# A hybrid attention block on one Trainium2 core: other order of the first chunks, gates computed earlier, low parts ahead of sums, one GpSimd product on VectorE

## The chip, the cores and the metric

The kernel runs on one core of a Trainium2 chip. The core's engines work side by side, each through its own queue in order: TensorE (PE: matmuls, and the loading of their weights, PEld), VectorE (DVE), ScalarE (ACT), GpSimd (POOL) and SyncE (SP), which here issues nearly all DMA transfers. The metric is the time of one execution on the device, in microseconds; less is better. Before the change it is 2038.04 us, the median of three runs (2036.83 to 2039.37).

## The reference

One residual layer over 512 tokens of width 2048, in float32. Heads are 128 wide, eight of each kind.

```python
h = rmsnorm(x, g_attn)
proj = h @ w_in                        # qa, ka, va, qf, kf, vf, f_logit
log_f = log_sigmoid(f_logit + b_f)
o_sb  = stick_breaking_attention(qa, ka, va)
o_fox = forgetting_attention(qf, kf, vf, log_f)   # scores + c_t - c_s, c = cumsum(log_f)
x = x + concat(headnorm(o_sb), headnorm(o_fox)) @ w_out
u = relu(rmsnorm(x, g_mlp) @ w_up)
y = rmsnorm(x + (u * u) @ w_down, g_final)
```

## The kernel before, in words

**Precision.** Each float32 operand is split into a high part, rounded to the matmul's format (`fp32r`), and a low part, the rest. ScalarE makes the high part by a cast, VectorE the low part by a subtraction (`Piece.cast` L166, `Piece.low` L170, `split` L56). A product is three matmuls (`mm3`, L75 to L78): high by high, high by low, low by high. High and low parts of weights lie in three rotating slots (tags `wh`, `wl`, `hi_lo` L67), the raw weights, as they come from memory, in three slots of the tag `wraw` (`Piece.load`, L159). Whoever takes a slot waits until its last user is done.

**Order.** A `Plan` (L143) holds pairs of a planned time and a function, and runs them sorted by time. Inside a `manual_schedule` the named engines keep the order so written. From L184 to L601 that holds for TensorE, ScalarE, VectorE and SyncE; from L602 to L1040 for the first three only, and there the scheduler places SyncE's transfers itself. The planned times only order the work: each engine starts an instruction as soon as its operands are there.

**Value phase** (L209 to L599). Sixteen chunks of 128 columns of x are turned by TensorE (`turn_x`, four transposes into one PSUM bank), scaled and split into `hH` and `hL` (`x_high` L253 on ScalarE, `x_low` L256 on VectorE), with some further copies for the later products (`x_more`, `x_right`, `x_sum`). Each chunk is multiplied at once with its 264 columns of W_in, the values of the first two heads and the eight gate logits (`first_part` L290, `first_values` L296): twelve matmuls a chunk. The order of chunks is 0, 8, 1, 9, 2, 10, and so on (`seq`, L301); chunks 0, 8, 1, 9 have a raw weight tile each, later ones a tile for the pair k, k + 8, all in `wraw` slots. `begin` (L310) is SyncE's list of first loads, of x and weights by turns. `keep_busy` (L286) puts matmuls without use on TensorE. Then the values of the other heads follow in two groups of seven products each, with sums of quadrants in place of the eighth (L415 to L599). In the second group, which begins at the planned time TV + END, each product takes four pieces of weights: a cast on ScalarE, a low part and for four of the seven products sums on VectorE. SyncE stores the results to `vd` (`added`, L520). Two pieces of the first head's query and one of its key are loaded and split here too (`first_pieces`, L208).

**Attention phase** (L602 to L1040). Its period is TPER = 27.05 us for each of 16 heads (order: forget heads 6, 7, 0 to 5, then the stick-breaking ones). In period n TensorE projects query and key of head n from four pieces of W_in (`q_piece`, `project` L199; pieces of head n have n and a = 0 to 3 in the loop from L961), computes scores of head n - 1 and the product with values of head n - 2. In the first period the plan also has the gates (L647 to L679): from the gate logits the log-forget sums, `cq` by rows, and `ckd` in memory, from which each forget head reads `cb`. Beside it W_out is loaded, summed and split for later (`WeightSums` L873, `whole` L911 for the first four row groups, `half` L924); these sums and low parts are VectorE's, and `whole` keeps its quadrants in `mixed`, over the place of value-phase tiles.

**Tail** (L1800 to L1895). The last row block: four products of 512 columns, the last in two halves; for each, VectorE adds the residual, ScalarE squares, and GpSimd multiplies by `g_final` (L1824), but for the last, which VectorE multiplies in halves (L1826). Then comes the row's norm and the store.

Of the kernel before, what the change touches and what calls it, by code (L numbers as in the profile page):

```python
# [8 lines left out]
F32 = mybir.dt.float32  # L9
# [27 lines left out]
def block_kernel(ctx, tc, x, g_attn, w_in, b_f, g_out_sb, g_out_fox, w_out, g_mlp, w_up, w_down, g_final, y):  # L37
# [167 lines left out]

    first_pieces = [q_piece(0, which, half) for which, half in ((0, 0), (0, 1), (1, 0))]
    with ExitStack() as stage:
# [96 lines left out]
        pieces = {}  # L304
        for j in (0, K8, 1, K8 + 1):
            pieces[j] = Piece(w_rows[j % K8][:, j // K8:j // K8 + 1, c0:c0 + m], 1, m), 0
# [8 lines left out]
        for k in range(K8):  # L315
            t, j = mm_at[k], k + K8
            for jj, dt in ((k, 0.0), (j, step)):
                if k == 0:
                    for part, wait in zip(("hh", "hl", "lh"), (0.0, 0.6, 1.1)):
                        plan.at(t + dt + wait, first_part, jj, *pieces[jj], part)  # L320
                    continue
# [3 lines left out]
            if k == 0:  # L325
                w8 = pieces[8][0]
                jobs = [(-64.5, keep_busy, 9), (-5.0, turn_x, k), (-4.9, keep_busy, 3), (-4.1, w.cast), (-4.0, x_high, k),
                        (-3.9, w.low), (-3.5, x_low, k), (-3.3, x_more, k), (0.1, turn_x, j), (0.2, w8.cast), (0.25, x_high, j),
                        (0.3, w8.low), (0.4, x_low, j), (0.6, x_sum, j), (0.85, x_right, j)]
            elif k == 1:  # L330
                w9 = pieces[9][0]
                jobs = [(-1.9, turn_x, k), (-1.85, w.cast), (-1.8, x_high, k), (-1.6, w.low), (-1.5, x_low, k), (-0.75, x_more, k),
                        (-0.8, turn_x, j), (-0.4, w9.cast), (-0.3, x_high, j), (0.3, w9.low), (0.4, x_right, j), (0.85, x_low, j), (1.6, x_sum, j)]
            else:
                dt = mm_at[k - 1] - t
                jobs = [(-2.95, turn_x, k), (-2.2, x_high, k), (-1.5, x_low, k), (-0.75, x_more, k),
                        (-1.02, turn_x, j), (-0.3, x_high, j), (0.4, x_right, j), (0.85, x_low, j), (1.6, x_sum, j),
                        (dt - 1.5, w.cast), (dt - 0.05, w.low)]
                if k > 3:
                    jobs.append((-14.0, w.load))  # L340
            for dt, f, *args in jobs:
                plan.at(t + dt, f, *args)
# [183 lines left out]
        r1s = [None]  # L526

# [74 lines left out]
    manual = tc.manual_schedule(engines={pe.engine, act.engine, dve.engine})  # L602
    manual.__enter__()
# [10 lines left out]
    with tc.tile_pool(name="att", bufs=1, side="right", reuse_waits="tile") as at, \  # L614
# [6 lines left out]
        utri = at.tile([P, P], F32R, name="utri")  # L621
        onesr = at.tile([P, P], F32R, name="onesr")
        rb = at.tile([P, NT], F32, name="rb")
        cq = at.tile([P, TB, NH], F32, name="cq")
        lf = at.tile([P, TB, 2 * NH], F32R, name="lf")
        fe = at.tile([P, TB, NH], F32, name="fe")
        r1, fl = r1s[0], gates
# [3 lines left out]
        tri = at.tile([P, P], F32, tag="uh5", name="tri")  # L631
        pool.memset(tri, 0.0)
        pool.affine_select(out=tri, in_=tri, compare_op=ALU.is_gt, fill=1.0, base=0, pattern=[[-1, P]], channel_multiplier=1)
        one = at.tile([P, P], F32, tag="ul5", name="one")
        pool.memset(one, 1.0)
# [10 lines left out]

        def gates_1():  # L647
            for t in range(TB):
                dve.scalar_tensor_tensor(fl[:, t, :], fl[:, t, :], r1[:, t:t + 1], bf, op0=ALU.mult, op1=ALU.add)
            dve.tensor_copy(utri, tri)  # L650
            dve.tensor_copy(onesr, one)

        def gates_2():
            act.activation(fe, fl, AF.Abs)
            act.activation(fe, fe, AF.Exp, scale=-1.0)
            act.activation(fe, fe, AF.Ln, bias=1.0)
            dve.scalar_tensor_tensor(fl, fl, 0.0, fe, op0=ALU.min, op1=ALU.subtract)
            split(lf[:, :, :NH], lf[:, :, NH:], fl)

        def gates_3():  # L660
            cps = now["cps"] = atp.tile([P, TB, 2 * NH], F32, tag="o", name="cps")
            for t in range(TB):
                for i in range(t + 1):
                    pe.matmul(cps[:, t, :], utri if i == t else onesr, lf[:, i, :], start=(t == 0 and i == 0),
                              stop=(i == t), skip_group_check=True)

        def gates_4():
            act.copy(cq, now["cps"][:, :, :NH])
            dve.tensor_tensor(cq, cq, now["cps"][:, :, NH:], op=ALU.add)

        def gates_5():
            cT = now["cT"] = atp.tile([P, NT], F32, tag="o", name="cT")
            for t in range(TB):
                pe.transpose(cT[:NH, t * P:(t + 1) * P], cq[:, t, :], ident)

        def gates_6():
            ckT = at.tile([NH, NT], F32, tag="ul4", name="ckT")
            act.mul(ckT, now["cT"][:NH, :], -1.0)
            sp.dma_start(ckd, ckT)  # L679
# [50 lines left out]
        class Head:  # L730
# [41 lines left out]
            def plan_fox(self, plan, t):  # L772
# [28 lines left out]
                for dt, f in ((-4.0 if self.i else -1.5, load), (10.85, start), (14.6, maxed), (16.8, soft), (20.1, scale)):  # L801
                    plan.at(t + dt, f)
# [108 lines left out]
        def whole(m, t):  # L911
            w = WeightSums(m, (0, 1), lambda: mixed[:, :NH].rearrange("p (q a) n -> p q (a n)", a=2))
            loads, first, second = ((-15.0, 2.7), (21.5, 22.3, TPER + 3.3), (TPER + 1.75, TPER + 2.5, TPER + 6.7)) if m else \
# [6 lines left out]
            for dt, f in ((second[2] + 0.1, lambda: w.store(0, 2)), (TPER + 9.2, lambda: w.sum(2)), (TPER + 17.5, lambda: w.sum(3)),  # L920
                          (2 * TPER + 1.75, w.high_6), (2 * TPER + 2.5, w.low_6), (2 * TPER + 2.6, lambda: w.store(2, 4))):
                plan.at(t + dt, f)

        def half(m, d, n):  # L924
# [3 lines left out]
            jobs = [(17.6 if n == 8 else 8.3, w.load)]  # L928
            if d == 0:
                c, a = (23.2, (1.75, 2.4, 3.1, 3.8, 5.6, 6.4)) if n > 7 else (16.4, (5.5, 6.3, 7.0, 9.0, 12.0, 17.4))  # L930
                jobs += [(c, lambda: w.high(0)), (c + 0.7, lambda: w.low(0)), (c + 1.2, lambda: w.sum(0)), (c + 2.0, lambda: w.sum(1))]
# [29 lines left out]
        for n in range(2 * NH + 1):  # L961
            t = TPER * n
            i_s, i_o = n - 1, n - 2
            if n < 2 * NH:
                pieces = []
                for a, (which, hf) in enumerate(((0, 0), (0, 1), (1, 0), (1, 1))):
# [4 lines left out]
                    if n == 1 and a == 0:  # L971
                        cast, low = -7.0, -5.0
                    if n == 0:
                        cast, low = 16.3, 18.2
                    pieces.append(q_piece(n, which, hf).plan(plan, t + cast - 16, t + cast, t + low))
# [25 lines left out]
            if 0 <= i_s < 2 * NH:  # L1001
# [29 lines left out]
        for dt, f in ((16.25, widen_r1), (17.0, turn_r1), (17.5, lambda: act.copy(rb, now["rb"])), (17.1, gates_1), (17.9, gates_2), (21.5, gates_3),  # L1031
                      (22.0, gates_4), (24.2, gates_5), (24.8, gates_6)):
# [7 lines left out]
    manual.__exit__(None, None, None)  # L1040

    up_cm.__exit__(None, None, None)
    for cm in acc_cms[::-1]:
        cm.__exit__(None, None, None)
# [763 lines left out]
    def last_product(t, n, *banks):  # L1808
# [9 lines left out]
        for j, (ps, cols) in enumerate(zip(banks, parts)):  # L1818
# [4 lines left out]
            if len(parts) == 1:  # L1823
                pool.tensor_tensor(x2_, x2_, gf[:, n * NT:(n + 1) * NT], op=ALU.mult)  # L1824
            else:
                scaled = dve.tensor_tensor(last_piece[:, cols], x2_, gf[:, n * NT:(n + 1) * NT][:, cols], op=ALU.mult)  # L1826
# [10 lines left out]
    def last_row(t):  # L1837
# [20 lines left out]
        else:  # L1858
            m = [x2(t, 0), x2(t, 1), x2(t, 2), last_piece]
# [19 lines left out]
    last_piece = spare.tile([P, NT], F32, name="last")  # L1879
# [60 lines left out]
```

## Time and profile before

| | |
|---|---|
| median of three runs | 2038.04 us |
| lowest, highest | 2036.83, 2039.37 us |
| the profiled execution | 2037.16 us |
| its span, first to last instruction | 2035.1 us |
| TensorE busy | 2017.4 us, 99% of the span |
| VectorE busy | 1739.8 us, 85% |
| ScalarE busy | 1128.1 us, 55% |
| GpSimd busy | 64.5 us, 3% |
| mean granted TensorE clock | 0.998 |

All stretches and moments below are of the profiled execution, in us from the first instruction. A row of the timeline has the start, the duration, the engine, the line, the operation, the output, its inputs and the count; in brackets stands the idle time of the engine just before it and what ended it. "PE accq L78 <- DVE wl L171: 2.5, 1, 2.5" in the list of waits is: TensorE at L78 waited for VectorE's L171, 2.5 us in total, once, 2.5 at the longest. In the windows view each engine's busy time is followed by its count of instructions, and the last three columns are the granted clock, the busy share of the DMA engines and GB/s.

### The profile page before, as it was taken

The page shows a single profiled execution, that of the slowest core. Times are in us where ns is not written, and L with a number is a line of the kernel's source. Part 1 is how long each engine was busy: PE and PEld are TensorE (multiplying, and loading weights), DVE is VectorE, ACT ScalarE, POOL GpSimd, SP SyncE. Part 2 cuts the span into 40 slices and gives each one's busy share as a digit, 9 for nine tenths or more (in the row PEclk, how much of TensorE's full clock was granted, in tenths as well). Part 3 has the DMA queues.
Part 4 walks back from the last instruction along what each step waited for, and adds up shares of the span by engine and source line. Part 5 has one row for each costly group of instructions (what it writes and reads, how often), then busy time and mean ns, then how long its engine had stood idle before and what let it go on. Part 6 is the DMA issues. An engine that isn't in the chain of part 4 may idle for free.

```text
span 2035.1 us, 27208 instructions
## 1 busy us (share of the span) xinstructions
PE 2017.4 (99%) x10422; PEld 1744.6 (86%) x10422; DVE 1739.8 (85%) x1969; ACT 1128.1 (55%) x1619; POOL 64.5 (3%) x73
## 2 busy tenths in 40 slices
PE   8999999999999999999999999999999999999998
PEld 8998888888888889888888888888888888888887
DVE  7876777888867588899999999998799888888896
ACT  6543454455555566667667677676644344444444
POOL 0000001100000000000000000000000000000004
PEclk9999999999999999999999999999999999999999
DMA  6426666666538981766666666667685674674642
GB/s 225 164 98 221 198 203 189 211 202 197 183 119 278 301 268 65 234 182 187 211 207 189 215 193 211 198 197 257 241 299 197 225 260 169 235 253 176 222 162 85
DMA packets 270210, 413.45 MB, mean 203 GB/s; under 512 B 10312, under 2 KB 166008, under 8 KB 263552
## 3 DMA queue, kind: packets, MB, share of 16 engines
q1 hardware_dynamic: 269328, 409.61, 60.7%
q8 instruction: 82, 1.34, 0.3%
q10 hardware_dynamic: 752, 2.11, 0.3%
q14 instruction: 48, 0.39, 0.1%
HBM read 315.19 MB, written 96.49 MB: 202 GB/s over the span
## 4 chain that ended last, share of the span: by engine, by line
PE 93%; DVE 3%; DMA 1%; ACT 1%; issue 1%; POOL 0%; SPq 0%; ACTq 0%; POOLq 0%; DVEq 0%
PE psa L1175 10%; PE accd L77 8%; PE accd L78 8%; PE accd L76 8%; PE accq L76 5%; PE accq L78 5%; PE accq L77 5%; PE psa L1173 5%; PE psc L1175 5%; PE psc L1173 3%; PE psb L1175 3%; PE m L77 1%; PE m L76 1%; PE m L78 1%; PE psb L1173 1%; PE vy L78 1%
## 5 line engine op out<-in xcount | busy, mean ns | idle before, releaser
L1752 ACT CAST wh<-wd 128x1024 fp32r<-128x1024 f32 x126 | 124.9, 999 | 169.3 <-PE accd L78 54.6
L1642 DVE TENSOR_TENSOR wl<-wu,wh 128x1024 fp32r<-128x1024 f32 x158 | 192.6, 1220 | 13.0 <-ACT wh L1636 13.0
L78 PE MATMUL accq<-hH,wl 128*128 128x512 f32 x512 | 200.6, 392 | 2.5 <-DVE wl L171 2.5
L76 PE MATMUL accq<-hH,wh 128*128 128x512 f32 x512 | 202.2, 395 | 0.0
L77 PE MATMUL accq<-hL,wh 128*128 128x512 f32 x512 | 200.3, 391 | 0.0
L1636 ACT CAST wh<-wu 128x1024 fp32r<-128x1024 f32 x158 | 167.4, 1060 | 44.8 <-issue 22.6
L1175 PE MATMUL psa<-f,wh 128*128 128x512 f32 x720 | 179.0, 391 | 0.0
L77 PE MATMUL accd<-wl,uf 128*128 128x512 f32 x436 | 169.6, 389 | 0.0
L78 PE MATMUL accd<-wh,uf 128*128 128x512 f32 x436 | 169.6, 389 | 0.0
L76 PE MATMUL accd<-wh,uf 128*128 128x512 f32 x436 | 169.4, 389 | 0.0
L1175 PEld LDWEIGHTS psa<-f,wh 128*128 128x128 f32 x720 | 132.3, 188 | 25.6
L1759 DVE TENSOR_TENSOR wl<-wd,wh 128x1024 fp32r<-128x1024 f32 x126 | 144.0, 1152 | 10.6 <-ACT wh L1752 10.6
L1524 DVE TENSOR_TENSOR m<-m,accd 128x1024 f32<-128x1024 f32 x84 | 102.2, 1217 | 46.1 <-PE accd L78 46.1
L1752 ACT CAST wx<-wd 128x1024 fp32r<-128x1024 f32 (+1 forms) x82 | 80.8, 994 | 106.3 <-PE accd L78 40.5
L78 PEld LDWEIGHTS accq<-hH,wl 128*128 128x128 f32 x512 | 96.6, 189 | 23.2 <-DVE wl L171 2.9
L168 ACT CAST wh<-wraw 128x1024 fp32r<-128x1024 f32 (+2 forms) x78 | 76.8, 987 | 66.8 <-PE accq L77 50.2
L76 PEld LDWEIGHTS accq<-hH,wh 128*128 128x128 f32 x512 | 96.7, 189 | 18.6
L77 PEld LDWEIGHTS accq<-hL,wh 128*128 128x128 f32 x512 | 96.5, 189 | 18.7
L76 PE MATMUL accd<-wx,uf 128*128 128x512 f32 x284 | 110.5, 389 | 0.0
L77 PE MATMUL accd<-wx,uf 128*128 128x512 f32 x284 | 110.5, 389 | 0.0
L78 PE MATMUL accd<-wx,uf 128*128 128x512 f32 x284 | 110.5, 389 | 0.0
L1173 PEld LDWEIGHTS psa<-f,wl 128*128 128x128 f32 x720 | 96.0, 191 | 5.9 <-ACT l L1206 0.6
(442 smaller groups left out, 5104.2 us busy)
## 6 DMA issues: line engine op xcount, KB each, us to landing
wu<-in_w_up_dram SPq DMA_DIRECT2D x60, 1024.0 KB, 6.5
ufd<-st SPq DMA_DIRECT2D x98, 512.0 KB, 4.3
wd<-in_w_down_dram SPq DMA_DIRECT2D x48, 1024.0 KB, 7.9
uf<-ufd SPq DMA_DIRECT2D x42, 1024.0 KB, 7.2
wraw<-in_w_in_dram SPq DMA_DIRECT2D x68, 512.0 KB, 4.1
wo<-wsums SPq DMA_DIRECT2D x28, 512.0 KB, 4.9
q<-in_w_in_dram SPq DMA_DIRECT2D x32, 384.0 KB, 5.6
wd<-in_w_down_dram SPq DMA_DIRECT2D x16, 768.0 KB, 6.4
```

Source lines behind the costliest of these rows:

```text
L76: pe.matmul(out, sh, mh, start=first, stop=False, skip_group_check=True)
L77: pe.matmul(out, sh, ml, start=False, stop=False, skip_group_check=True)
L78: return pe.matmul(out, sl, mh, start=False, stop=last, skip_group_check=True)
L168: act.copy(self.hi, self.source())
L1173: ins = pe.matmul(ps[:, 2 * P:], lo[:, a, :], f_parts(p, a)[0], start=False, stop=last, skip_group_check=True)
L1175: ins = pe.matmul(ps, hi[:, a, :], f_both(p, a), start=a == PAIRS[0] and p in (1, 5), stop=last, skip_group_check=True)
L1524: dve.tensor_tensor(M[p][:, :, db, :], M[p][:, :, db, :], ps, op=ALU.add)
L1636: act.copy(rooms[k][0], srcs[k])
L1642: lows[0] = dve.tensor_tensor(lo, srcs.pop(k), hi.bitcast(F32), op=ALU.subtract)
L1752: act.copy(rooms[k + 3][0], srcs[k + 3])
L1759: dve.tensor_tensor(rooms[k + 2][1], srcs.pop(k + 2), rooms[k + 2][0].bitcast(F32), op=ALU.subtract)
```

## The change

1. First chunks. The order becomes 0, 1, 8, 9, then 2, 10, 3, 11 and so on. The weights of 0, 1, 8, 9 come in two transfers into one tile of their own (`e3`); the pairs of chunks 2 to 5 have places in that tile and in `e4`; only those of 6 and 7 use `wraw`. SyncE's first list is shorter by one and in another order. Five filler matmuls stand where there were three, and one more ahead of them.
2. Gates. The work of L632 to L679 moves into the value phase, to planned times TV + END + 26 to 42. `onesr` and `cq` get a pool of their own; the rest uses the tiles `e3` and `e4`.
3. Start of the attention phase. SyncE's order is written out there too, up to the planned time 52. The second head's pieces (n == 1) are loaded, cast and split at other times; the first W_out group's (m == 0) loads, splits and sums, and some loads and one sum of others, move.
4. Tail. The product of the third 512 columns of the last row block goes from GpSimd to VectorE, into a tile of its own.

```diff
-        seq = [j for k in range(K8) for j in (k, k + K8)]
-        t0, step = 6.5, 1.93
+        seq = [0, 1, K8, K8 + 1] + [j for k in range(2, K8) for j in (k, k + K8)]
+        t0, step = 5.9, 1.93
...
+        early_w = [vf.tile([P, K8 * 2 * P], F32, tag=f"e{i}", name="wfirst")[:, :6 * m].rearrange("p (a b) -> p a b", b=m) for i in (3, 4)]
+        for i, j in enumerate((0, 1, K8, K8 + 1)):
+            pieces[j] = Placed(early_w[0][:, i:i + 1]), 0
         for k in range(2, K8):
-            w = Piece(w_rows[k][:, :, c0:c0 + m], 2, m)
+            if k < 6:
+                room[k] = early_w[0][:, 4:6] if k == 2 else early_w[1][:, 2 * k - 6:2 * k - 4]
+                w = Placed(room[k])
+            else:
+                w = Piece(w_rows[k][:, :, c0:c0 + m], 2, m)
...
-        begin = [(load_x, 0, 1), (pieces[0][0].load,), (load_x, 8, 2), (pieces[8][0].load,), (load_x, 1, 1),
-                 (pieces[1][0].load,), (load_x, 2, 2), (pieces[9][0].load,), (load_x, 10, 2), (pieces[2][0].load,),
-                 (load_x, 4, 4), (pieces[3][0].load,), (load_x, 12, 4)]
+        begin = [(load_x, 0, 1), (load_first_w, 0), (load_x, 1, 1), (load_x, 8, 2), (load_first_w, 1), (load_x, 2, 2), (load_w, 2),
+                 (load_x, 10, 2), (load_w, 3), (load_x, 4, 4), (load_w, 4), (load_x, 12, 4)]
...
+        for dt, f in ((26.0, gates_0), (30.0, gates_1), (31.0, gates_2), (37.0, gates_3), (38.5, gates_4), (40.5, gates_5), (42.0, gates_6)):
+            plan.at(TV + END + dt, f)
...
-    manual = tc.manual_schedule(engines={pe.engine, act.engine, dve.engine})
+    manuals = [tc.manual_schedule(engines={pe.engine, act.engine, dve.engine, sp.engine})]
...
             loads, first, second = ... if m else \
-                ((16.4, 16.5), (TPER + 1.75, TPER + 2.5, TPER + 3.3), (TPER + 5.8, TPER + 6.6, TPER + 7.3))
+                ((20.5, 20.6), (TPER + 1.75, TPER + 2.5, TPER + 4.5), (TPER + 10.0, TPER + 10.7, TPER + 7.0))
...
-                    if n == 1 and a == 0:
-                        cast, low = -7.0, -5.0
+                    load = cast - 16 if n != 2 or a else -21.4
+                    if n == 1:
+                        load = -23.0 if a == 0 else load
+                        cast, low = ((-7.0, -5.0), (-3.0, -2.0), (2.9, 3.9), (8.5, 9.5))[a]
...
-                    plan.at(t - 12.0, load_v, p_)
+                    plan.at(t - 12.0 if p_ else t + 3.0, load_v, p_)
...
+        plan.at(52.0, free_loads)
...
-            if len(parts) == 1:
+            if (t, n) == (TB - 1, 2):
+                dve.tensor_tensor(last_pieces[0], x2_, gf[:, n * NT:(n + 1) * NT], op=ALU.mult)
+            elif len(parts) == 1:
                 pool.tensor_tensor(x2_, x2_, gf[:, n * NT:(n + 1) * NT], op=ALU.mult)
```

`Placed` is a `Piece` whose raw weights lie in a given place; `load_first_w(s)` loads the pair 0, 1 or 8, 9 and `load_w(k)` the pair k, k + 8; `free_loads` ends the written order for SyncE and goes on with that for the other three engines. In each three-number group of `whole` the times are those of the high part, the low part and the sum; before, the second head's low parts a = 1 and 2 stood at 5.4 and 10.9 of the period, its a = 3 at 13.95.

More of the change, by code (lines that the diff above doesn't have):

```diff
@@ L313, in block_kernel @@
         for i, (f, *args) in enumerate(begin):
             plan.at(-50 + i, f, *args)
-        for k in range(K8):
+        for j in seq[:4]:
+            for part, wait in zip(("hh", "hl", "lh"), (0.0, 0.6, 1.1)):
+                plan.at(mm_at[j] + wait, first_part, j, *pieces[j], part)
+        plan.at(-58.0, keep_busy, 9)
+        plan.at(-54.5, keep_busy, 1)
+        plan.at(1.0, keep_busy, 5)
+        early = {0: ((-5.0, turn_x), (-4.1, "cast"), (-4.0, x_high), (-3.9, "low"), (-3.5, x_low), (-3.3, x_more)),
+                 1: ((-1.83, turn_x), (-1.8, "cast"), (-1.75, x_high), (-1.7, "low"), (-1.6, x_low), (-1.5, x_more)),
+                 8: ((-1.16, turn_x), (-1.1, "cast"), (-1.05, x_high), (-1.0, "low"), (-0.9, x_low), (-0.5, x_sum), (-0.4, x_right)),
+                 9: ((-2.59, turn_x), (-1.9, "cast"), (-1.85, x_high), (-1.6, x_right), (-1.5, "low"), (-1.4, x_low), (-1.3, x_sum))}
@@ L316, in block_kernel @@
+        for j, jobs in early.items():
+            for dt, f in jobs:
+                if isinstance(f, str):
+                    plan.at(mm_at[j] + dt, getattr(pieces[j][0], f))
+                else:
+                    plan.at(mm_at[j] + dt, f, j)
+        for k in range(2, K8):
             t, j = mm_at[k], k + K8
             for jj, dt in ((k, 0.0), (j, step)):
[L318 to L321, printed above, removed]
@@ new lines, in gates_1, with gates_2 @@
+        def gates_1():
+            for t in range(TB):
+                dve.scalar_tensor_tensor(gates[:, t, :], gates[:, t, :], r1s[0][:, t:t + 1], bf, op0=ALU.mult, op1=ALU.add)
+            dve.tensor_copy(gate["utri"], gate["tri"])
+            dve.tensor_copy(onesr, gate["one"])
+        def gates_2():
+            fe, lf = gate["fe"], gate["lf"]
+            act.activation(fe, gates, AF.Abs)
+            act.activation(fe, fe, AF.Exp, scale=-1.0)
+            act.activation(fe, fe, AF.Ln, bias=1.0)
+            dve.scalar_tensor_tensor(gates, gates, 0.0, fe, op0=ALU.min, op1=ALU.subtract)
+            split(lf[:, :, :NH], lf[:, :, NH:], gates)
@@ new lines, in gates_3, with gates_4 @@
+        def gates_3():
+            ps = gate["ps"] = accs[0].tile([P, NT], F32, tag="acc", name="cps")
+            cps = gate["cps"] = ps[:, :TB * 2 * NH].rearrange("p (t n) -> p t n", t=TB)
+            for t in range(TB):
+                for i in range(t + 1):
+                    pe.matmul(cps[:, t, :], gate["utri"] if i == t else onesr, gate["lf"][:, i, :], start=(t == 0 and i == 0),
+                              stop=(i == t), skip_group_check=True)
+        def gates_4():
+            act.copy(cq, gate["cps"][:, :, :NH])
+            dve.tensor_tensor(cq, cq, gate["cps"][:, :, NH:], op=ALU.add)
@@ L645, in turn_r1 @@
                 pe.transpose(now["rb"][:, t * P:(t + 1) * P], now["rw"][:, t * P:(t + 1) * P], ident)
[L647 to L679, printed above, removed]
         def scale_u(i, which):
```

110 lines of the change are left out of this document (66 added, 44 removed).

## The prediction

> **What bounds the kernel now.** I read the page first; of its 2035.1 us span the chain that ended last is made of:
>
> ```profile
> PE 93%; DVE 3%; DMA 1%; ACT 1%; issue 1%; POOL 0%; SPq 0%; ACTq 0%; POOLq 0%; DVEq 0%
> ```
>
> TensorE carries 93% of the chain, and the change takes no matmul away. So it can only win where TensorE stands still. The windows view of the first 20 us (TensorE busy is the number after the window's length; the last two columns are DMA share and GB/s) and the list of what TensorE waited for, longest first, say where:
>
> ```profile
> 0.00:5.00 5.00, 3.42 (x15) 3.16 (x16) 1.17 (x4) 1.70 (x2) 0.74 (x7) 1.00 0.46 125
> 5.00:10.00 5.00, 3.93 (x29) 3.43 (x28) 2.86 (x5) 1.77 (x3) 0.00 (x0) 1.00 1.00 311
> 10.00:15.00 5.00, 4.01 (x30) 3.34 (x28) 1.97 (x4) 1.82 (x4) 0.00 (x0) 1.00 1.05 343
> 15.00:20.00 5.00, 3.30 (x25) 3.10 (x26) 4.12 (x7) 3.43 (x8) 0.00 (x0) 1.00 1.01 375
> ```
>
> ```profile
> PE accq L78 <- DVE wl L171: 2.5, 1, 2.5
> PE vy L76 <- ACT hH L254: 1.8, 1, 1.8
> ```
>
> Two places, then: the first 20 us, and one wait of 2.5 us for a low part (`wl`). A third is the tail, where the chain leaves TensorE. I work them in this order.
>
> **Part 1, the first chunks.** The timeline of TensorE gives the marks: the first product of chunk 0, and two successive chunks once it runs dense.
>
> ```profile
> 5.91 0.51 PE L294 MATMUL vy<-wh,hH 128*128 128x264 f32 x2
> ...
> 18.94 0.36 PE L76 MATMUL vy<-wh,hH 128*128 128x264 f32 x1
> ...
> 20.83 0.37 PE L76 MATMUL vy<-wh,hH 128*128 128x264 f32 x1
> ```
>
> A chunk with its transposes takes 20.83 - 18.94 = 1.89 us. At 20.83 five chunks are done, begun at 5.91; dense they take 5 x 1.89 = 9.45 us, and one more turn of four transposes (some 0.45, an estimate: 1.89 less twelve products at 0.12) makes 9.9. So 20.83 - 5.91 - 9.9 = **5.0 us** is all there is to win here.
>
> Why the stall? SyncE issues its tenth load, chunk 2's weights, late:
>
> ```profile
> 8.78 0.38 SPq L161 DMA_DIRECT2D wraw<-in_w_in_dram  x1
> ```
>
> ```profile
> 14.54 0.94 ACT L168 CAST wh<-wraw 128x528 fp32r<-128x528 f32 x2 [3.01 <-DMA wraw<-in_w_in_dram]
> ```
>
> They waited on SyncE for one of three `wraw` slots and land at 14.54. ScalarE, in order, holds chunk 9's `hH` behind that cast, and TensorE waits 1.84 for it. With own tiles nothing on SyncE waits for a slot; twelve loads at 0.4 to 0.5 us each (this row has 0.38) issue by about 6.5 us, and TensorE takes 0, 1, 8, 9 in place of 0, 8, 1, 9.
>
> What is late next is the pair of weights for 8 and 9, fifth in the queue. Up to it lie 256 + 264 + 256 + 512 + 264 KB, 1.59 MB; by the windows above 0.63 MB have moved at 5 us and 311 GB/s follow, so its bytes are through at 8.1. How much later it lands I bound by chunk 2's load: up to it lay 2.91 MB, through at 12.1 by the same rows, landed 14.54, so 2.4 late. It lands between 8.1 and 10.5; I take 10.0, nearer that row. Then a cast, about 0.4 (a third of the two above by columns, and some start-up), and one `hH`, 0.7:
>
> ```profile
> 5.17 0.69 ACT L254 ACTIVATE hH<-tr,g_in 128x512 fp32r<-128x512 f32 x1 [0.70 <-PE tr L251]
> ```
>
> Chunk 8 begins at 11.2. By then chunks 0 and 1 are done. From there three chunks (8, 9, 2) are 5.7 us dense; I add 0.7 for ScalarE, which has three casts, three `hH` and two right halves to do in a row for them. Chunk 10 begins at 17.6 where it began at 20.83: **3.2 us** won. Bounds: 5.0 above; below, 1.5 (the pair lands 1 us later still, and another 0.7 of waits). Chunk 0's weights are now twice as large and may land up to 0.6 later; that hides behind the wait for chunk 8. The five filler matmuls replace three and end before `hH` of chunk 0 is there.
>
> **Part 2, the gates in the value phase.** The same instructions move 30 us earlier on TensorE, ScalarE and VectorE: on TensorE nothing is won or lost. They bring a wait into VectorE's queue:
>
> ```profile
> 170.05 1.14 DVE L523 SCALAR_TENSOR_TENSOR s<-vz,r1v,s 128x384 f32<-128x384 f32 x2 [1.81 <-PE vz L78]
> ...
> 171.65 0.63 DVE L649 SCALAR_TENSOR_TENSOR gates<-gates,r1v,bf 128x8 f32<-128x8 f32 x4
> ...
> 173.42 0.19 DVE L657 SCALAR_TENSOR_TENSOR gates<-gates,fe 128x32 f32<-128x32 f32 x1 [0.87 <-ACT fe L656]
> 173.90 0.19 DVE L59 TENSOR_TENSOR lf<-gates,lf 128x32 fp32r<-128x32 f32 x1 [0.28 <-ACT lf L58]
> 174.01 1.22 DVE L171 TENSOR_TENSOR wl<-wraw,wh 128x1024 fp32r<-128x1024 f32 x1
> ```
>
> From 171.65 on that is 174.01 - 171.65 = 2.4 us in which the next low part waits. At the new place (END + 30, about 141 us) the value phase's lows queue behind, and TensorE waits for those. A cast of theirs on ScalarE, and the lows on VectorE:
>
> ```profile
> 140.97 0.84 ACT L168 CAST wh<-q 128x768 fp32r<-128x768 f32 x1 [1.23 <-PE vy L78]
> ```
>
> ```profile
> 141.84 0.96 DVE L171 TENSOR_TENSOR wl<-q,wh 128x768 fp32r<-128x768 f32 x1 [0.67 <-ACT wh L168]
> 142.72 1.75 DVE L428 TENSOR_TENSOR q<-q,q 128x1536 f32<-128x1536 f32 x1
> 144.39 0.95 DVE L171 TENSOR_TENSOR wl<-q,wh 128x768 fp32r<-128x768 f32 x1
> ```
>
> A cast starts when TensorE frees a slot, every 0.84 + 1.23 = 2.07 us; with three slots its piece is multiplied two periods later: this one at 145.1, the next at 147.2, the low part 0.3 after that. The two lows end at 142.8 and 145.3; 2.4 later, less the 0.7 that VectorE idles before the first, they end by 144.5 and 147.0. It holds, by 0.5. Cost taken: 0; bounds 0 and 0.7.
>
> **Part 3, low parts ahead of sums.** VectorE's queue ahead of the 2.5 us wait, the clock (third column from the end) just after it, one product's time in the chain, and the first product of the first head's last piece:
>
> ```profile
> 193.57 2.48 DVE L896 TENSOR_TENSOR mixed<-mixed 128x1024 f32<-128x1024 f32 x2
> 195.97 1.92 DVE L782 SCALAR_TENSOR_TENSOR w<-s,cq,cb 128x128 f32<-128x128 f32 x4
> 197.80 2.67 DVE L171 TENSOR_TENSOR wl<-wraw,wh 128x1024 fp32r<-128x1024 f32 x2
> ```
>
> ```profile
> 200.30:203.70 3.40, 3.40 (x9) 2.66 (x8) 3.05 (x7) 1.35 (x5) 0.00 (x0) 0.50 0.93 227
> ```
>
> ```profile
> 189.32 0.23 PE accq L76
> ```
>
> ```profile
> 177.12 0.48 PE L76 MATMUL accq<-hH,wh 128*128 128x512 f32 x1
> ```
>
> The first of the two lows, the second head's third piece, stands behind two sums and the softmax start; it ends at about 199.0, so TensorE wanted it 2.5 earlier, at 196.5. The change plans it at 3.9 us of the head's period, ahead of the sums (4.5 and 7.0) and of the second W_out low part (10.7). What it needs: a raw slot, free when the low of 174.01 ends (175.2), its load (5.8 us as chunk 2's, so 181), and a cast slot, free when TensorE ends the piece begun at 177.12: 24 products of 0.23 and the 0.4 of gate transposes, 183. Ahead of it stand one W_out cast and low, whose load waits for the value phase's last store as before. I put it before 190, an estimate with 6 us to spare. So the 2.5 us go, and with them the 3.40 us at clock 0.50, which lost half, 1.7: **4.2 us**. The fourth piece's low is late next: it is due 24 products later, at 202, and now stands ahead of the softmax start too. On SyncE, `vr` and the next head's pieces now stand behind the wait for the first W_out low part (some 187); the pieces are due a period after that, so it costs nothing, and if that cover went, a wait of the load's 5.8 us would show at 210. The other moved sums and loads stand under dense TensorE work; nothing.
>
> [...]
>
> **Part 4, the tail.**
>
> ```profile
> 2025.52 0.42 DVE L1820 TENSOR_TENSOR m<-m,acce 128x256 f32<-128x256 f32 x1 [0.75 <-PE acce L78]
> ...
> 2025.97 1.27 DVE L1826 TENSOR_TENSOR last<-m,gf 128x256 f32<-128x256 f32 x1
> ...
> 2027.29 0.40 DVE L1820 TENSOR_TENSOR m<-m,acce 128x256 f32<-128x256 f32 x1
> ...
> 2027.74 0.41 DVE L1826 TENSOR_TENSOR last<-m,gf 128x256 f32<-128x256 f32 x1
> ```
>
> The same product takes 1.27 beside a GpSimd product and 0.41 after it; without GpSimd, 0.86 less. The product put on VectorE (512 columns, about 0.7) fits into its 0.75 of idle time before 2025.52. The last sum then waits for TensorE: its half is twelve products of 0.12 after the first half's, 2025.52 + 1.44 = 2026.96 for 2027.29. Won **0.35**, bounds 0 and 0.86.
>
> **Sum.** The profiled execution took 2037.16 (0.88 under the median of three, inside their range). 2037.16 - 3.2 - 0 - 4.2 - 0.35 = **2029.4**; own range 2026.5 to 2032.
>
> **Rivals.**
> - *The handover.* SyncE's order is now written out in the attention phase too. The load of the first head's last piece, planned after the value phase, stood inside it, moved up by the scheduler:
>
> ```profile
> 163.31 0.46 SPq L161 DMA_DIRECT2D wraw<-in_w_in_dram  x1
> ```
>
> If it now follows the value phase's last store, behind the sums of 170.05 to 171.2 (172.7 with the gates ahead of them), it lands 5.8 us after its issue at 173, at 178.9; the cast (1.0) and the low (1.2, the row at 174.01) make 181.1. TensorE wants this piece at 177.12 + 0.4, its low 0.5 later: 3.1 us of stall, and 1.7 of clock if it falls: **2034.2**, 2032.5 without. For it: the order is by hand. Against: the load depends only on a free slot, and the old trace moved it up across the boundary.
> [...]
> - *Loads share the engines*: twelve at once, the early ones land as late as before; part 1 wins nothing, **2032.6**. For: chunk 2's load landed 2.4 after its bytes' turn, with 1 MB issued behind it. Against: SyncE's wait for a slot, which held chunk 2's load till 8.78, goes in any case.
> - *The other side, slower:* the same sharing in full. If the weights of 8 and 9 land only with all 5.55 MB, at about 19 by the windows' rates, chunk 8 begins at 20.1 and chunk 10 at 26.5, 5.7 later than now: 2037.16 + 5.7 - 4.2 - 0.35 = **2038.3**, and more with clock falls in the idle start (1.7 each). It decides from a landing at 13.3 (part 1 turns to a loss) and passes the old time at 17.9. Against: chunk 2's load, with 1 MB behind it, took 5.8 us from issue to landing, and this one issues at 3 us.
>
> **How the numbers follow.** Forecast 0.56; handover 0.17; clock 0.08; sharing 0.12; slower 0.07. A measurement of this kernel tells 0.2%, about 4 us, from no change. Faster by more: forecast and clock whole, 0.10 of sharing, 0.02 of handover: 0.76. Within: 0.15 of handover, 0.02 of sharing, 0.02 of the slower case: 0.19. Slower: 0.05. The range 2026.5 to 2035 takes in the forecast, the clock, sharing and the handover, and leaves out the slower case and some 0.1 of tails.
>
> **What would show it.** Part 1: ScalarE's `hH` wait of 1.8 is gone, and chunk 10's first product stands near 17.6. Part 2: no TensorE wait near 147. Part 3: the list of waits has no `accq <- wl`, and the clock is 1.00 from 190 to 210. Part 4: the first 256-column product takes 0.41. I am wrong if TensorE waits for `wraw` or `wl` near 178, or if chunk 8 begins after 14.

## The result, and the profile after

The changed kernel takes 2032.7 us (median of 12 runs, 2030.78 to 2036.59), the kernel before 2037.94 in the same comparison (12 runs, 2036.83 to 2039.37). The ratio is 0.9977, 95% interval 0.9969 to 0.9985: 4.7 us won (3.1 to 6.3), where the terms of the forecast came to 7.75. The time lies 0.7 above the forecast's own range (2026.5 to 2032) and inside the wide one that took in the rivals (to 2035), but for a reason that stood in neither. The profiled execution took 2033.73 us, with a span of 2032.0.

**The first 20 us.** The same views as before: TensorE's list of waits, longest first, and the windows.

```profile
PE o L77 <- DVE pl L862: 2.1, 1, 2.1
PE vx L293 <- DVE still L289: 1.6, 1, 1.6
PE psa L78 <- DVE wl L59: 0.9, 2, 0.5
PE o L76 <- ACT ph L859: 0.6, 1, 0.6
PE tr L256 <- DVE f L271: 0.5, 1, 0.5
PE tr L256 <- ACT x L268: 0.4, 1, 0.4
```

```profile
5.00:10.00 5.00, 4.88 (x39) 4.65 (x38) 3.94 (x7) 2.49 (x6) 0.00 (x0) 1.00 1.01 316
10.00:15.00 5.00, 4.04 (x33) 3.56 (x31) 3.00 (x6) 3.79 (x8) 0.00 (x0) 1.00 1.06 394
15.00:20.00 5.00, 5.00 (x41) 4.89 (x42) 4.48 (x8) 3.47 (x7) 0.00 (x0) 1.00 1.07 395
```

The wait of 1.8 for `hH` is gone, and so is TensorE's idle time from 15 to 20. The marks of TensorE's timeline (chunk 0, chunk 8, chunk 10), and ScalarE at the weights of chunk 8:

```profile
6.23 0.51 PE L299 MATMUL vy<-wh,hH 128*128 128x264 f32 x2
...
10.66 0.51 PE L299 MATMUL vy<-wh,hH 128*128 128x264 f32 x2
...
17.90 0.37 PE L76 MATMUL vy<-wh,hH 128*128 128x264 f32 x1
```

```profile
8.90 0.41 ACT L168 CAST wh<-wfirst 128x264 fp32r<-128x264 f32 x1 [0.75 <-DMA wfirst<-in_w_in_dram]
```

The weights landed at 8.9, chunk 8 began at 10.66 and chunk 10 at 17.90, where it began at 20.83 before: 2.93 us won.

**From 140 to 215 us.** Nothing is lost where the gates went, nor near 178 (windows again):

```profile
140.00:170.00 30.00, 30.00 (x177) 29.26 (x176) 21.07 (x27) 13.66 (x20) 0.00 (x0) 1.00 0.25 64
170.00:180.00 10.00, 10.00 (x46) 8.35 (x47) 5.20 (x8) 3.21 (x4) 0.00 (x0) 1.00 1.01 310
```

The 2.5 us for the low part `wl` near 199 are gone as well. In their place stand the first line of the list above, 2.1 us for `pl`, and 0.6 for `ph`: the low and high part of the first head's softmax weights. TensorE and VectorE there, and the clock just after:

```profile
201.54 1.25 PE L850 MATMUL pt<-ident,w 128*128 128x128 f32 x10
...
205.15 0.61 PE L78 MATMUL accq<-hH,wl 128*128 128x512 f32 x2
206.35 0.51 PE L76 MATMUL o<-ph,vh 128*128 128x512 f32 x1 [0.58 <-ACT ph L859]
208.93 0.50 PE L77 MATMUL o<-pl,vh 128*128 128x512 f32 x1 [2.08 <-DVE pl L862]
```

```profile
200.15 0.18 DVE L838 RECIPROCAL ml<-ml 128x4 f32<-128x4 f32 x1 [2.42 <-ACT w L835]
200.36 1.28 DVE L840 TENSOR_SCALAR w<-w,ml 128x128 f32<-128x128 f32 x4
201.55 1.22 DVE L171 TENSOR_TENSOR wl<-wraw,wh 128x1024 fp32r<-128x1024 f32 x1
202.69 1.22 DVE L937 TENSOR_TENSOR mixed<-mixed 128x1024 f32<-128x1024 f32 x1
203.82 0.69 DVE L728 SCALAR_TENSOR_TENSOR qf<-accq,rb 128x512 f32<-128x512 f32 x1
205.20 0.69 DVE L736 TENSOR_TENSOR ul<-qf,uh 128x512 fp32r<-128x512 f32 x1 [0.69 <-ACT uh L732]
205.81 1.67 DVE L758 SCALAR_TENSOR_TENSOR vl<-vr,r1v,vh 128x256 fp32r<-128x256 f32 x4
207.39 1.48 DVE L862 TENSOR_TENSOR pl<-pt,ph 128x1280 fp32r<-128x1280 f32 x1
```

```profile
210.00:211.00 1.00, 1.00 (x9) 1.00 (x7) 0.84 (x2) 0.65 (x2) 0.00 (x0) 0.64 0.91 321
211.00:212.00 1.00, 1.00 (x4) 0.81 (x4) 0.46 (x1) 0.71 (x2) 0.00 (x0) 0.50 0.50 194
```

Read VectorE's rows from the first: it waits 2.42 us for the softmax on ScalarE, and from then on it is full but for 0.69. `pl` is the last of a chain in which a low part for the third head (201.55), a sum of W_out (202.69), the scaled query and its low part, and the low part of the values all stand ahead of it. ScalarE's `ph` is late by the same chain: it stands behind `uh`, which waits for `qf`. Before, the same queue stood like this, and TensorE came later:

```profile
202.16 1.22 DVE L896 TENSOR_TENSOR mixed<-mixed 128x1024 f32<-128x1024 f32 x1
204.67 0.18 DVE L797 RECIPROCAL ml<-ml 128x4 f32<-128x4 f32 x1 [1.29 <-ACT w L794]
...
211.11 1.49 DVE L821 TENSOR_TENSOR pl<-pt,ph 128x1280 fp32r<-128x1280 f32 x1 [0.25 <-ACT ph L818]
```

```profile
208.56 1.25 PE L809 MATMUL pt<-ident,w 128*128 128x128 f32 x10
...
213.32 0.39 PE L77 MATMUL o<-pl,vh 128*128 128x512 f32 x1
```

TensorE now turns the softmax weights at 201.54 in place of 208.56, 7.0 us earlier: 2.9 of part 1, 2.5 of the wait that is gone, 1.7 of the half-rate stretch (3.40 us at clock 0.50) that is gone. VectorE's `pl` begins only 3.7 earlier, at 207.39 in place of 211.11. And the sum, which stood inside the wait for the softmax before (202.16, ahead of the reciprocal), now stands behind it. So TensorE idles 0.58 + 2.08 = 2.66 us, and the clock is 0.50 behind that, from 210.28 (the window's 0.64 is 0.28 at 1 and 0.72 at 0.50) to 213.68: the 2.5 + 1.7 that part 3 took away are paid again 10 us later.

**The tail.** VectorE's last rows:

```profile
2022.77 0.42 DVE L1877 TENSOR_TENSOR last<-m,gf 128x256 f32<-128x256 f32 x1
...
2023.75 0.42 DVE L1869 TENSOR_TENSOR m<-m,acce 128x256 f32<-128x256 f32 x1 [0.43 <-PE acce L78]
```

The first 256-column product takes 0.42 for 1.27, and the last sum waits for TensorE. TensorE's last product begins at 2023.43 (2026.63 before), so the last sum follows it by 0.32 in place of 0.66: 0.34 won there. It can't be seen at the end of the span, though: that lies 8.57 us behind this product, for 8.47 before.

### The profile page after: what moved, and what is told of

Same layout as the page of the kernel before. It is cut to its first block, busy times and chain, and to the rows that moved or that the text cites. A ratio compares the mean times of both kernels' runs of the same rounds, so it can differ in the third digit from the quotient of the medians.

```text
span 2032.0 us, 27211 instructions
## 1 busy us (share of the span) xinstructions
PE 2017.1 (99%) x10425; PEld 1745.0 (86%) x10425; DVE 1739.4 (86%) x1970; ACT 1128.0 (56%) x1619; POOL 63.4 (3%) x72
## 4 chain that ended last, share of the span: by engine, by line
PE 93%; DVE 3%; DMA 1%; ACT 1%; issue 1%; POOL 0%; SPq 0%; ACTq 0%; POOLq 0%
PE psa L1224 10%; PE accd L78 8%; PE accd L76 8%; PE accd L77 8%; PE psa L1222 5%; PE accq L76 5%; PE accq L78 5%; PE accq L77 5%; PE psc L1224 5%; PE psc L1222 3%; PE psb L1224 3%; PE m L78 1%; PE m L77 1%; PE m L76 1%; PE psb L1222 1%; PE vy L78 1%
## 5 line engine op out<-in xcount | busy, mean ns | idle before, releaser
L168 ACT CAST wh<-wraw 128x1024 fp32r<-128x1024 f32 (+1 forms) x70 | 72.7, 1040 | 63.2 <-PE accq L77 51.3
```

The lines of the kernel that those rows point to most:

```text
L168: act.copy(self.hi, self.source())
```

## The experiments

Each kernel is the changed one or the one before with one edit. Two theories stood against each other after this profile. **Theory:** the order of VectorE's queue behind the softmax makes the new wait, so moving single instructions out of it takes it away. **Rival:** VectorE is simply full from 185 to 220, and whatever is moved, a stall of that size turns up. A second question was what each part is worth by itself. The table has the results; the kernel before was measured beside each (2037.8 to 2038.0). "Waits" are TensorE's from 185 to 215 in the profile, in us.

| kernel | median (lowest to highest, runs) | ratio, 95% interval | waits |
|---|---|---|---|
| changed | 2032.7 (2030.78 to 2036.59, 12) | 0.9977, 0.9969 to 0.9985 | 0.58 + 2.08 |
| changed, again | 2032.16 (2030.42 to 2035.21, 10) | 0.9975, 0.9966 to 0.9984 | 2.09 |
| part 1 alone | 2033.59 (2032.85 to 2035.97, 11) | 0.9981, 0.9972 to 0.9990 | 2.37 + 0.45 |
| part 2 alone | 2037.7 (2035.59 to 2039.99, 11) | 1.0001, 0.9993 to 1.0010 | 2.35 + 1.42 + 0.42 |
| part 3 alone | 2038.45 (2036.12 to 2041.97, 11) | 1.0006, 0.9997 to 1.0014 | 0.64 + 0.69 + 2.09 |
| part 4 alone | 2036.94 (2035.54 to 2039.68, 11) | 0.9998, 0.9989 to 1.0007 | 1.80 + 0.43 |
| without part 1 | 2035.88 (2034.23 to 2039.54, 11) | 0.9995, 0.9986 to 1.0004 | 1.11 |
| without part 3 | 2034.12 (2033.36 to 2036.01, 11) | 0.9984, 0.9975 to 0.9993 | 1.71 + 1.30 + 0.45 |
| sum behind `pl` | 2030.99 (2030.76 to 2032.31, 5) | 0.9969, 0.9956 to 0.9981 | 1.91 |
| sum and low part behind `pl` | 2030.75 (2030.17 to 2031.01, 5) | 0.9965, 0.9953 to 0.9978 | 1.83 |
| filled gap | 2029.67 (2029.0 to 2031.38, 5) | 0.9963, 0.9950 to 0.9975 | none |
| filled gap, more fillers | 2029.10 (2028.89 to 2029.98, 5) | 0.9959, 0.9947 to 0.9972 | none |

**Sum behind `pl`.** The fourth sum of the first W_out group is planned behind the weights' low part.

```diff
-... (TPER + (17.5 if m else 21.0), lambda: w.sum(3)), ...
+... (TPER + (17.5 if m else 26.5), lambda: w.sum(3)), ...
```

> The changed kernel with one VectorE sum moved: the fourth sum of the first W_out group, which stands ahead of the second head's scaled query (1.22 us in the trace), goes behind the first head's low weights `pl`. Theory (the order of VectorE's queue makes the new wait): everything behind the sum comes 1.2 us earlier, `pl` ends at about 207.65 in place of 208.87, the wait for `ph` (0.6) goes and the wait for `pl` falls from 2.1 to about 1.3; together TensorE idles some 1.3 in place of 2.66. If the half-rate stretch needs the longer idle time it goes too: 2032.7 - 1.3 - 1.7 = 2029.7. Rival 1 (VectorE is full in this stretch, the wait only moves on): another wait of about 1.2 appears within the next 20 us and the time stays near 2032.7. Rival 2 (the clock falls anyway): 2031.4.

The wait for `ph` went, that for `pl` fell to 1.91 only, and no half-rate stretch followed (clock 1.00 from 200 to 220). In this execution the softmax began 1.14 us later than in the changed kernel's (193.73 for 192.59), behind the W_out split ahead of it, so that the query's scaling stood at 203.83 as before. By the medians 1.2 to 1.7 us are won; the intervals overlap. The theory had a wait of 1.3 and, without a half-rate stretch, 2029.7: the direction fits, the sizes do not, and the rival is not yet excluded.

**Sum and low part behind `pl`.** The low part of the third head's first piece, too, beside the edit above.

```diff
+                    if n == 2 and a == 0:
+                        low = -0.9
```

> As the kernel with the moved sum, and the low part of the third head's first piece (1.22 us on VectorE) stands behind `pl` too. Theory: `pl` ends 2.4 us earlier than in the changed kernel, at about 206.4, before TensorE wants it (206.85); no wait for `ph` or `pl`, clock 1.00 from 190 to 220: 2032.7 - 2.7 - 1.7 = 2028.3. Rival 1 (VectorE is full): the low part of the third head's first piece is then late at about 208.6, TensorE waits 0.5 to 1.5 for `wl`, and the time is 2030 to 2032. Rival 2 (the clock falls anyway): 2030.0.

`pl` went to 204.68 and no product waited for it. But this low part was needed sooner than I had taken: one step of the third head's first piece stands ahead of the product `o` in TensorE's order. The list of waits and VectorE's row:

```profile
PE accq L78 <- DVE wl L171: 1.8, 1, 1.8
```

```profile
206.08 1.21 DVE L171 TENSOR_TENSOR wl<-wraw,wh 128x1024 fp32r<-128x1024 f32 x1
```

That is the rival's sign: behind the softmax there is too much due at once, and putting one thing back brings another forward. What is left is the time ahead of it, the 2.42 us in which VectorE waits for ScalarE.

**Filled gap.** The sum and that low part go into the wait for the softmax, and the values' low part into the 0.69 in which VectorE waits for `uh`.

```diff
-... (TPER + (17.5 if m else 21.0), lambda: w.sum(3)), ...
+... (TPER + 17.5, lambda: w.sum(3)), ...
...
+                    if n == 2 and a == 0:
+                        low = -11.1
...
-plan.at(t + (6.3 if i_s >= NH else 23.65), low_v, p_)
+plan.at(t + (6.3 if i_s >= NH else 23.65 if i_s else 22.8), low_v, p_)
```

> The changed kernel, three VectorE instructions moved: the fourth sum of the first W_out group and the low part of the third head's first piece go into the 2.42 us in which VectorE waits for the softmax (L835), where 2.44 us of work fit; the low part of the first head's values goes ahead of the low part of the scaled query, into the 0.69 in which VectorE waits for `uh`. Theory (the order of VectorE's queue after the softmax makes the wait): `pl` ends near 206.0, before TensorE wants it at 206.0 to 206.6; no wait for `ph`, `pl` or `wl` over 0.5 from 185 to 220, clock 1.00 there. Against the kernel with the low part behind `pl` (2030.75, wait 1.83): 2029.0. Rival 1 (VectorE is full from 185 to 220 and a stall of some 1.8 turns up elsewhere): 2030.8. Rival 2 (the low part in the gap delays the softmax's scale, as its cast is late on ScalarE): a wait for `ph`, 2030 to 2032.

VectorE's timeline, then the windows:

```profile
197.36 0.17 DVE L831 TENSOR_SCALAR ml<-ml 128x4 f32<-128x4 f32 x1
197.47 1.23 DVE L171 TENSOR_TENSOR wl<-wraw,wh 128x1024 fp32r<-128x1024 f32 x1
198.62 1.22 DVE L937 TENSOR_TENSOR mixed<-mixed 128x1024 f32<-128x1024 f32 x1
199.96 0.18 DVE L838 RECIPROCAL ml<-ml 128x4 f32<-128x4 f32 x1
...
204.48 1.49 DVE L862 TENSOR_TENSOR pl<-pt,ph 128x1280 fp32r<-128x1280 f32 x1 [0.25 <-ACT ph L859]
```

```profile
185.00:200.00 15.00, 15.00 (x71) 12.59 (x71) 12.00 (x18) 6.71 (x16) 1.73 (x2) 1.00 1.06 345
200.00:220.00 20.00, 20.00 (x102) 16.82 (x101) 16.10 (x27) 8.78 (x12) 2.16 (x2) 1.00 0.76 256
```

The 2.42 us are used up, the reciprocal starts without a wait, `pl` is done at 205.97, and TensorE is busy for all 35 us at the full clock. No wait of TensorE stands in the list from 185 to 300 us, so the stall did not move on either. VectorE had the room; the order had left it empty. By the trace the rival falls. The time alone would not settle it: 2029.67 lies 2.5 to 3.0 below the changed kernel's two medians, but the interval is nearly that of the kernel with sum and low part behind `pl` (0.9950 to 0.9975, 0.9953 to 0.9978). It is within 0.3 of what the prediction had summed for the change, here with three more instructions moved.

**Without part 3.** First chunks, gates and tail changed; the plan of the attention phase as before.

```diff
-    manuals = [tc.manual_schedule(engines={pe.engine, act.engine, dve.engine, sp.engine})]
+    manuals = [tc.manual_schedule(engines={pe.engine, act.engine, dve.engine})]
...
-                ((20.5, 20.6), (TPER + 1.75, TPER + 2.5, TPER + 4.5), (TPER + 10.0, TPER + 10.7, TPER + 7.0))
+                ((16.4, 16.5), (TPER + 1.75, TPER + 2.5, TPER + 3.3), (TPER + 5.8, TPER + 6.6, TPER + 7.3))
...
-                        cast, low = ((-7.0, -5.0), (-3.0, -2.0), (2.9, 3.9), (8.5, 9.5))[a]
+                    if n == 1 and a == 0:
+                        cast, low = -7.0, -5.0
```

> The changed kernel with the start of the attention phase as before (order of low parts, sums and loads, SyncE left to the scheduler); first chunks, gates and tail stay changed. Theory (part 3 only moved the stall): the wait for the low part is back near 193 with about 2.5 us, the wait for `pl` is gone, the half-rate stretch follows it: the same time as the changed kernel, 2032.0 to 2034.0. By my prediction's sum (part 3 wins 4.2): 2036.9. The gates gone from the queue could shorten the wait by up to 2.4: then 2030.5.

2034.12: the waits for `wl` are back, now two (1.71 and 1.30), the one for `pl` is 0.45. So with parts 1, 2 and 4 in place, part 3 is worth 1.4 us by the medians, and its interval overlaps with the changed kernel's. The medians are far from a worth of 4.2.

**Part 3 alone.** The plan of the attention phase on the kernel before. The load of `cb` for the first head stays at its old time, since the gates come later here. The edit is the last one turned round:

```diff
-    manual = tc.manual_schedule(engines={pe.engine, act.engine, dve.engine})
+    manuals = [tc.manual_schedule(engines={pe.engine, act.engine, dve.engine, sp.engine})]
...
+                        cast, low = ((-7.0, -5.0), (-3.0, -2.0), (2.9, 3.9), (8.5, 9.5))[a]
...
```

> The kernel before with the start of the attention phase changed alone: low parts ahead of sums, SyncE's order by hand; first chunks, gates and tail as before. Theory (part 3 removes the wait for `wl` and makes one for `pl` of about its size): front wait of 1.8 still there, no `accq <- wl` of 2.5 but 2 to 3 us for `pl` near 210; 2036.5 to 2038.0, that is 0 to 1.5 less than before. By my prediction's sum: 2033.8. Rival (without the gates out of the way SyncE's or VectorE's order is worse): over 2038.5.

```profile
PE o L77 <- DVE pl L826: 2.1, 1, 2.1
...
PE o L76 <- ACT ph L823: 0.7, 1, 0.7
PE pt L814 <- DVE w L804: 0.6, 1, 0.6
```

1.0006 (0.9997 to 1.0014): nothing won, perhaps something lost. The wait for `wl` is gone and 3.4 us of waits stand in its place, with a half-rate stretch behind them (0.50 from 213.58 to 217.00). This shows the exchange by itself, without any help of part 1.

**Part 1 alone, and all but part 1.** The first chunks of the change put into the kernel before, and taken out of the changed one.

```diff
-        seq = [j for k in range(K8) for j in (k, k + K8)]
-        t0, step = 6.5, 1.93
+        seq = [0, 1, K8, K8 + 1] + [j for k in range(2, K8) for j in (k, k + K8)]
+        t0, step = 5.9, 1.93
...
```

> The kernel before with the first chunks changed alone. Theory: chunk 10's first product at 17.9, 2.9 us earlier than before, and all later work shifts with it: 2037.9 - 2.9 = 2035.0. Rival (what follows the front hangs on loads that do not come earlier, so the wait of 2.5 near 196 grows): between 2035.0 and 2037.9, with a longer `accq <- wl` wait.

> The changed kernel with the first chunks as before; gates, attention start and tail stay changed. If part 1 is worth the same with the other parts as alone (2038.0 - 2033.6 = 4.4 alone, of which 2.9 at the front in the trace): 2032.4 + 2.9 to 4.4 = 2035.3 to 2036.8, waits for `pl` of 2.1 and for `hH` of 1.4 to 1.8. Rival (parts 2 and 3 win nothing by themselves, the front decides): 2037.8. [...]

Alone it wins 3.9 us by the ratio (2.0 to 5.7), with the wait for `wl` at 2.37, no longer than before. Without it the other three leave 1.0 (a gain of 2.9 to a loss of 0.8), with 1.11 of wait for `pl` and the old wait for `hH` back, 2.03. Of the change's 4.7, then, most is part 1, as far as intervals this wide can say.

**Part 2 alone, part 4 alone.** The one edit or the other in the kernel before.

```diff
+        for dt, f in ((26.0, gates_0), (30.0, gates_1), (31.0, gates_2), (37.0, gates_3), (38.5, gates_4), (40.5, gates_5), (42.0, gates_6)):
+            plan.at(TV + END + dt, f)
...
```

```diff
+            if (t, n) == (TB - 1, 2):
+                dve.tensor_tensor(last_pieces[0], x2_, gf[:, n * NT:(n + 1) * NT], op=ALU.mult)
...
```

> The kernel before with the gates in the value phase alone. By my prediction: 0, so 2038.0, no TensorE wait near 147. Theory from the traces with and without the gates moved (1.7 + 1.3 in place of 2.4 of waits for `wl`): +0.6, 2038.5. Rival (2.4 us of VectorE's queue freed at 171 to 174 pull the late low part earlier): the wait of 2.5 shrinks, 2035.5 to 2037.

> The kernel before with the tail's GpSimd product on VectorE alone. Theory: the first 256-column product at 0.42 in place of 1.27, the last sum 0.34 earlier against TensorE's end: 2038.0 - 0.35 = 2037.65, within the noise of the runs. Rival (VectorE's product delays the third column block's chain): 2038.0 or above, and the last sum still 0.4 or more behind TensorE's end than in the changed kernel.

Neither can be told from no change. Of part 2 the trace says a little more: the low parts near 193 and 200 wait twice, 2.35 + 1.42, in place of once. The tail's 0.34 shows in the trace and is too small for these runs.

**Changed, again.** The same kernel without an edit, for the clock.

> The changed kernel once more, for the clock. In its profile the clock fell to 0.50 from 210.9 to 214.3 after waits of 0.58 and 2.08; in the kernel with the first chunks alone a wait of 2.37 cost no clock. [...] Rival (the fall hangs on the total idle time of this place): the clock falls again at the same place, for 3.4 us, span 2032.0.

The clock fell again, at 211.82, for 210.28 in the first profile (the 210.9 above was misread), for 3.42 us; the span was 2033.5. But this execution also began otherwise (see the section on the hardware), and the wait for `ph` was missing, so that TensorE idled 2.09 here in place of 2.66 and the run doesn't decide what the fall hangs on.

**Filled gap, more fillers.**

```diff
-        plan.at(1.0, keep_busy, 5)
+        plan.at(1.0, keep_busy, 7)
```

> The kernel with the filled gap, and seven filler matmuls in place of five ahead of chunk 0, to close the idle tenths of a us in which TensorE waits for the first `hH`. [...]

All five runs lie below 2030.0, and this is the fastest kernel here: 0.9959 of the one before (0.9947 to 0.9972), 8.4 us. Against the filled gap alone the intervals overlap, so what the two fillers add isn't settled: in the one profile of each the products are fast from the first on (two in 0.41 at 6.52 with them, in 0.51 at 6.16 without) and chunk 8 begins at 10.85 with them, at 10.81 without.

## Why the prediction was right and wrong

**Part 1 was right, with some luck in the number.** Forecast 3.2, measured 2.93 in the trace and 3.9 (2.0 to 5.7) by itself. The weights for 8 and 9 landed at 8.9, inside the bounds of 8.1 to 10.5 and before the 10.0 that I took. Chunk 8 began at 10.66 (11.2). That was given back by what I had as a lump of 0.7: from chunk 8 to chunk 10 it took 7.24 for my 6.4, and the transposes waited 0.4 and 0.5 there for the copies that read the PSUM bank. Chunk 10 stood at 17.90 (17.6): an early landing and a slower stretch behind it nearly cancel. The loads did not slow each other down: 316 and 394 GB/s from 5 to 15 us, where it was 311 and 343. Both rivals on shared transfers fall.

**Part 2 and part 4 were right at their places.** No wait near 147; 0.42 for the first product and 0.34 at the last sum, forecast 0.35. Neither shows in the time: the tail's gain is not there at the end of the span, and the gates alone left more waits for `wl` near 193 and 200, which the prediction did not look at.

**Part 3 was wrong, and with it the sum.** Its first half held: the low part came in time and the 2.5 us went. The step that failed is "the other moved sums and loads stand under dense TensorE work; nothing". I asked what is late next only of the same kind, the fourth piece's low part, and I looked at the moved sums from TensorE's side. From VectorE's side one of them left a place that cost nothing (inside the wait for the softmax) for one that cost all of its 1.22 us. And I took 4.2 us off TensorE's time without asking whether VectorE could deliver that much earlier as well. In this order it could not: 3.7 of 7.0 (with the filled gap `pl` began 6.6 earlier). The row that would have told was at hand: `pl` began at 211.11 and was used at 213.32, with 0.7 to spare behind its 1.49. Any gain beyond 0.7 on TensorE ahead of it had to be won on VectorE too.

**The rivals.** The handover did not happen: no wait near 178. The 0.08 for the clock stands for a fall without a wait ahead of it, and no run shows one: in each of the five profiles with a fall on the way it came behind a wait of TensorE, in the changed kernel from 210.28, 1.35 after the 2.08 for `pl` had ended. The price, half of 3.40 us, was 1.7. That 2032.7 is just what sharing (2032.6) and the handover without its clock fall (2032.5) gave is chance: part 1 won its 2.93, and there was no stall near 178. The slower side had 0.07 and did not come. That a wait for another operand would take the place of the one removed, in the same stretch, was not among the rivals, although the time it gives (2037.16 - 3.2 - 0.35 = 2033.6) needs no new number. The profiled execution took 2033.73.

## What to carry to other kernels

When a stall goes, everything that TensorE wants behind it is wanted earlier; list for each operand in the next 20 us when it was ready and when it was used, and the smallest of these margins (here 0.7 us, of `pl`) bounds the gain until the engine that makes it is relieved too. Look where that engine waits (here 2.42 us for the softmax) and put work with a free due time there; an instruction moved out of such a wait can cost its whole length (here the sum's 1.22 us), though no engine shows as the bound. And measure parts alone as well as left out: here one of four made most of the gain.

## What the runs showed of the hardware

**At the start the same two products took 0.81 us in one execution and 0.51 in another.** TensorE's timeline in the second profile of the changed kernel (compare 6.23 and 10.66 in the first):

```profile
6.62 0.81 PE L299 MATMUL vy<-wh,hH 128*128 128x264 f32 x2
...
9.84 0.64 PE L299 MATMUL vz<-wh,hL 128*128 128x264 f32 x2
10.28 0.49 PE L299 MATMUL vy<-wh,hH 128*128 128x264 f32 x2
...
12.71 0.52 PE L299 MATMUL vy<-wh,hH 128*128 128x264 f32 x2
```

The same pair of products takes 0.81 at 6.62 and 0.49 at 10.28, though the granted clock shows 1.00 from 0 to 20. In the first profile it took 0.51 already at 6.23. Chunk 8 came 2.05 later for it, at 12.71, and that run was the slowest of its ten (2035.21). What sets the moment, no run shows.

**Five of the thirteen profiles have one stretch at clock 0.50 on the way, 3.40 to 3.42 us long.** In this second profile it begins here:

```profile
211.00:212.00 1.00, 1.00 (x8) 0.95 (x7) 0.31 (x2) 0.91 (x2) 0.00 (x0) 0.91 0.91 306
```

0.91 puts the fall at 211.82, and the 0.88 from 215 to 216 its end at 215.24. In the first profile it lies from 210.28 to 213.68, in the kernel before from 200.34 to 203.74, in part 3 alone from 213.58 to 217.00, and without part 1 from 17.96 to 21.38, behind the old wait for `hH`. These five profiles have a mean granted clock of 0.998, the other eight 0.999. Products of 512 columns begin 0.43 apart in it (first profile, from 211.52) and 0.23 apart ahead of it (from 204.70). The fall without part 1:

```profile
17.31 0.39 PE L76 MATMUL vy<-wh,hH 128*128 128x264 f32 x1 [2.03 <-ACT hH L259]
```

```profile
17.00:18.00 1.00, 0.57 (x2) 0.37 (x2) 0.79 (x3) 1.00 (x3) 0.00 (x0) 0.98 1.05 409
18.00:19.00 1.00, 0.54 (x2) 0.54 (x3) 1.00 (x3) 0.20 (x1) 0.00 (x0) 0.50 1.10 369
```

In every profile the clock is below 1 once more at the end (0.90 to 0.93 as the mean from 2000 to 2040), when TensorE has nothing left to do; in the first profile of the changed kernel and in the second here:

```profile
2026.00:2027.00 1.00, 0.00 (x0) 0.00 (x0) 0.96 (x4) 0.85 (x2) 0.00 (x0) 0.58 0.00 0
```

```profile
2027.00:2028.00 1.00, 0.00 (x0) 0.00 (x0) 0.92 (x4) 0.37 (x1) 0.00 (x0) 0.86 0.00 0
```

That is 2026.16 and 2027.72. From fall to fall it is 2026.16 - 210.28 = 1815.88 and 2027.72 - 211.82 = 1815.90, the same within 0.02, though both falls lie over 1.5 later in the second. In the kernel before it is 2029.88 - 200.34 = 1829.54, 13.65 more. What fixes these moments, no run shows.

**The length of the idle time alone doesn't tell whether the clock falls.** In the 3.41 us ahead of the five falls on the way TensorE had idled 2.03 (without part 1), 2.07 (changed), 2.09 (again), 2.14 (before) and 2.78 (part 3 alone): the part of the waits that lies in that stretch. Part 1 alone waited longer than most of these in one piece, and its clock stayed at 1.00 from 185 to 220:

```profile
196.19 0.50 PE L78 MATMUL accq<-hH,wl 128*128 128x512 f32 x1 [2.37 <-DVE wl L171]
```

Nor did the 2.35 in one piece of part 2 alone, at 193.36, bring a fall, nor the 1.91 of the kernel with the sum behind `pl`. So a wait of 2.03 came with a fall and one of 2.37 without; what else decides, no run shows, and no kernel was built to test it. Where the clock fell, the wait cost 1.7 us more (half of 3.40 to 3.42). That may be a part of why the changed kernel's runs spread over 5.8 us and the five of the filled gap over 2.4: the mean granted clock is 0.999 in the changed kernel's fastest runs and 0.997 in its two slowest, and 0.999 in all of the filled gap's. The two slowest have no profile, so it is not shown.
